# A seven-product block scheme for the gate and up products of an encoder's feed-forward layers

## The chip, the cores and the metric

The kernel runs on one core of a Trainium2 chip. The metric is the device time of one execution in microseconds (us). The engines work side by side, each through its own queue in order: TensorE (PE in the profile, its weight loads PEld), VectorE (DVE), ScalarE (ACT), GpSimd (POOL), and SyncE (SP), which here only issues transfers.

## The reference

Two macaron layers over 512 tokens of 1024 features. Each layer is a feed-forward block (FFN), a mixer of pooling, Fourier and attention heads, and a second FFN; a last norm follows. What the change touches is the FFN:

```python
D_MODEL, SEQ, DEPTH, D_FF = 1024, 512, 2, 2816

def rmsnorm(x, g):
    xf = x.astype(jnp.float32)
    y = xf * lax.rsqrt(jnp.mean(xf * xf, axis=-1, keepdims=True) + NORM_EPS)
    return (y * g.astype(jnp.float32)).astype(x.dtype)

def swiglu(x, w_gate, w_up, w_down):
    return (jax.nn.silu(x @ w_gate) * (x @ w_up)) @ w_down

for l in range(DEPTH):
    x = x + 0.5 * swiglu(rmsnorm(x, ffn1_norm[l]), ffn1_w_gate[l], ffn1_w_up[l], ffn1_w_down[l])
    x = x + mixers(rmsnorm(x, mix_norm[l])) @ w_out[l]
    x = x + 0.5 * swiglu(rmsnorm(x, ffn2_norm[l]), ffn2_w_gate[l], ffn2_w_up[l], ffn2_w_down[l])
```

## The kernel before, in words

Activations lie transposed: X[k] (k = 0 to 7) holds 128 features on the partitions and all 512 tokens along the free axis. Weights are the stationary operand of every projection. A float32 product is carried by three passes of float32r: each operand is split into a part hi and a rest lo, and hi x hi, hi x lo and lo x hi are added up in PSUM (mm3, L87). split() (L83) makes hi by a copy on ScalarE (L84) and lo by a subtraction on VectorE, in some places of the mixers on GpSimd (L85). The norm's gain is multiplied into x ahead of the product (Norm.scaled, L225); the factor per token, nm.r, is applied where sums leave PSUM. It comes from squares on ScalarE (L236), their sum on GpSimd (L240), two products with a matrix of ones and a chain of small VectorE steps (rsqrt, L183 to L209).

An FFN (ffn, L301) runs over two halves of the 2816 hidden features, 11 columns of 128 each. Per column a weight tile of 1 MB, gate and up side by side, is loaded and split, and pair() (L291) makes 2 x 8 x 3 matmuls of 128x128 by 128x512 into two PSUM banks. Then VectorE multiplies both banks by nm.r (L317, L319), ScalarE takes Silu (L318), VectorE multiplies gate by up (L320), and the result is split into ah and al. After 11 columns come eight down products (dn, L325 to L334) of 11 x 3 matmuls each, which are added to X[m]; in the second half each new X[m] is fed to the next norm at once.

The weights form one stream: weights() (L131) issues loads two items ahead and splits one item ahead. Staging has two buffers of 1 MB, hi and lo four of 0.5 MB each, work tiles 64 of 0.25 MB. [...] The mixers follow a list of steps written by hand (ORDER). [...]

Of the kernel before, what the change touches and what calls it, by code (L numbers as in the profile page):

```python
# [16 lines left out]
F32 = mybir.dt.float32  # L17
# [10 lines left out]
L = 2  # L28
DFF = 2816
NF = DFF // P  # L30
HALF = NF // 2
KT = D // P
NH = 4
# [4 lines left out]
NG = 64  # L38
# [9 lines left out]
# What runs on VectorE (or, for the row scale of the scores, ScalarE) rather than on GpSimd.  # L48
# [4 lines left out]
def build(tc, xt, gu, dn, qk, wv, wfa, wo, pw, fw, small, lamv, alibi, dft_c, dft_s, out):  # L53
# [3 lines left out]
    with (  # L57
        tc.tile_pool(name="const", bufs=1) as cp,
        tc.tile_pool(name="stage", bufs=2) as stp,
        tc.tile_pool(name="whi", bufs=4) as whp,  # L60
        tc.tile_pool(name="wlo", bufs=4) as wlp,
# [31 lines left out]
        items = []  # L93
        for l in range(L):
            for n in range(2):
                i = 2 * l + n
                if n:
                    src = {f"P{h}": qk[l, h] for h in range(NH)}
                    src |= {"V0": wv[l, 0], "V1": wv[l, 1], "A": wfa[l, 1], "F": wfa[l, 0]}
                    src |= {"W0a": wo[l, 0], "W1a": wo[l, 1], "W2": wo[l, 2], "W3": wo[l, 3]}  # L100
                    items += [(src[x], 2048, V if x in ON_VECTOR else G) for x in ORDER if x in src]
                for hf in range(2):
                    items += [(gu[i, hf * HALF + c], 2048, V) for c in range(HALF)]
                    items += [(dn[i, hf, m], HALF * P, V) for m in range(KT)]
        staged, ready = {}, {}
        pos = [0, 0, 0]

        def w_load(i, parts=1):
            src, w, _ = items[i]
            st = stp.tile([P, 2048], F32, tag="st", name=f"st{i}")  # L110
            q = w // parts
            for j in range(parts):
                nc.sync.dma_start(st[:, j * q : (j + 1) * q], src[:, j * q : (j + 1) * q])
            staged[i] = st

        def w_split(i, parts=1):
            _, w, eng = items[i]
            st = staged.pop(i)
            h = 1024 if w == 2048 else 6 * P
            res = []  # L120
            for n, (a, b) in enumerate(((0, h), (h, w))):
                hi = whp.tile([P, 1024], F32R, tag="hi", name=f"hi{i}_{n}")
                lo = wlp.tile([P, 1024], F32R, tag="lo", name=f"lo{i}_{n}")
                q = (b - a) // parts
                for j in range(parts):
                    s = slice(j * q, (j + 1) * q)
                    split(st[:, a + j * q : a + (j + 1) * q], hi[:, s], lo[:, s], eng)
                res += [hi, lo]
            ready[i] = res

        def weights():  # L131
            i = pos[0]
            pos[0] += 1
            while pos[1] < min(len(items), i + 3):
                w_load(pos[1])
                pos[1] += 1
            while pos[2] < min(len(items), i + 2):
                w_split(pos[2])
                pos[2] += 1
            return ready.pop(i)  # L140

# [4 lines left out]
        st0 = stp.tile([P, 2048], F32, tag="st", name="st0")  # L146
        for k in range(KT):
            nc.sync.dma_start(X[k], xt[k])
            if k % 2 == 0:
                s = slice(k * 256, (k + 2) * 256)  # L150
                nc.sync.dma_start(st0[:, s], items[0][0][:, s])
        staged[0] = st0
        pos[1] = 1
        w_load(1)
        pos[1] = 2
# [9 lines left out]
        # TensorE's clock rises while it works: products of zeros until the first weights are there.  # L165
# [11 lines left out]
        # 1/sqrt(-2 v): an exponent guess, a Newton step and a step of third order, scaled so that  # L177
        # each step ends in one (t + c) * y.
# [38 lines left out]
        class Norm:  # L217
# [7 lines left out]
            def scaled(self, k, act=False):  # L225
                gain = sm[:, self.c + k : self.c + k + 1]
                self.h[k], self.l[k] = g(F32R, name="xh"), g(F32R, name="xl")
                if act:
                    A.activation(self.h[k], X[k], AF.Copy, scale=gain)
                else:  # L230
                    V.tensor_scalar(self.h[k], X[k], gain, None, MUL)
# [15 lines left out]

        class Final:
            """The last RMSNorm: the sums over features as columns, tokens on partitions."""
# [41 lines left out]
        def pair(b, w, rh, rl, ks=range(KT), steps=((0, 4), (4, 7), (7, 8))):  # L291
            """Two tiles of outputs; k in the order of arrival, the last one at the end."""
# [8 lines left out]
        def ffn(nm, nxt, first=False):  # L301
            for hf in range(2):
                ah, alo = [], []
                for c in range(HALF):
                    w = weights()
                    b = [bank("gate"), bank("up")]
                    if first and hf == 0 and c == 0:
                        pair(b, w, nm.h, nm.l, steps=[(k, k + 1) for k in range(KT)])
                        for k in range(KT):
                            nm.squared(k)  # L310
                        held = b
                        continue
                    pair(b, w, nm.h, nm.l)
                    nm.end()
                    for b in [held, b] if first and hf == 0 and c == 1 else [b]:
                        t1, t2 = g(name="t1"), g(name="t2")
                        V.tensor_tensor(t1, b[0], nm.r, MUL)  # L317
                        A.activation(t1, t1, AF.Silu)  # L318
                        V.tensor_tensor(t2, b[1], nm.r, MUL)  # L319
                        V.tensor_tensor(t1, t1, t2, MUL)  # L320
                        h, lo = g(F32R, name="ah"), g(F32R, name="al")
                        split(t1, h, lo)
                        ah.append(h)
                        alo.append(lo)
                for m in range(KT):  # L325
                    w = weights()
                    b = bank("dn")
                    for j in range(HALF):
                        wh, wl = (w[0], w[1]) if j < 6 else (w[2], w[3])
                        s = slice((j % 6) * P, (j % 6 + 1) * P)  # L330
                        mm3(b, wh[:, s], wl[:, s], ah[j], alo[j], j == 0, j == HALF - 1)
                    V.scalar_tensor_tensor(X[m], b, 0.5, X[m], MUL, ADD)
                    if hf:
                        nxt.feed(m)  # L334

# [1 line left out]
        def mixer(l, nm, nxt):  # L337
# [131 lines left out]
            # pooling: window sums by doubling  # L469
# [45 lines left out]
            # Fourier: fold positions s and 512 - s, apply channels, then positions  # L515
# [117 lines left out]
        nm = Norm(C_FFN1)  # L633
        for k in range(KT):
            if k % 4 == 0:
# [109 lines left out]
```

## Time and profile before

| | |
|---|---|
| three runs | 1897.64, 1899.21, 1900.34 us; median 1899.21 us |
| span of the profiled execution | 1896.2 us; its time is not given apart from its span |
| TensorE busy | 1850.6 us (98%), 8057 matmuls |
| VectorE busy | 1034.7 us (55%) |
| ScalarE busy | 657.2 us (35%) |
| GpSimd busy | 162.9 us (9%) |
| HBM read | 168.82 MB, 90 GB/s over the span |

All durations come from one profiled execution, and sums are made against its span. In a row of groups stand the line, the engine, the operation, output and inputs by the program's names, the shape and the count, then total busy time in us and the mean of one in ns, then the idle time in front of them and what ended it. A row of the timeline starts with start and duration in us; several instructions merged into one row carry their count. In a row of stretches each engine's busy time stands with its number of instructions, and PEclk is the granted clock of TensorE as a share of full speed. An instruction that is held up while it runs shows a longer duration. A matmul's duration is its whole passage, and consecutive ones overlap.

### The profile page before, as it was taken

The numbers are of one execution on the slowest core, as the hardware profiler recorded it, in microseconds if no ns is written. First come the engines' busy times: TensorE is split into PE (matmuls) and PEld (weight loads), VectorE is DVE, ScalarE is ACT, GpSimd is POOL, SyncE is SP. The second block draws the span as 40 slices with busy tenths as digits, with TensorE's granted clock in tenths as the row PEclk, the third lists the DMA queues.
The fourth block names the chain that finished last, engine by engine and source line by source line (L and its number), as shares of the span: only waits on it lengthen the run. The fifth ranks groups of instructions, "written<-read, shape, count | busy, mean of one in ns | idle before, by whom it ended". The sixth has DMA issues, their size and how long they took to land.

```text
span 1896.2 us, 19973 instructions
## 1 busy us (share of the span) xinstructions
PE 1850.6 (98%) x8057; PEld 1496.7 (79%) x8057; DVE 1034.7 (55%) x1535; ACT 657.2 (35%) x960; POOL 162.9 (9%) x106
## 2 busy tenths in 40 slices
PE   9999999999799999999999999999998999999997
PEld 7888888877688888888888888888776888888886
DVE  6543444588788443444654334445988864334433
ACT  5322222367443222232322222322764432223232
POOL 2000000213211000000100000002232200000001
PEclk9999999999899999999999999999999999999998
DMA  5223222322103213222322232223221132232221
GB/s 193 107 72 113 93 97 74 114 86 92 45 23 114 109 61 108 109 89 77 112 101 93 76 120 89 84 90 111 86 70 45 67 111 82 77 120 89 87 87 60
DMA packets 31053, 172.21 MB, mean 91 GB/s; under 512 B 3568, under 2 KB 5616, under 8 KB 16752
## 3 DMA queue, kind: packets, MB, share of 16 engines
q1 hardware_dynamic: 27792, 167.25, 24.8%
q10 hardware_dynamic: 3168, 3.68, 0.6%
q8 instruction: 63, 1.03, 0.2%
q14 instruction: 30, 0.25, 0.0%
HBM read 168.82 MB, written 2.10 MB: 90 GB/s over the span
## 4 chain that ended last, share of the span: by engine, by line
PE 87%; DVE 8%; ACT 3%; issue 1%; DMA 0%; SPq 0%; DVEq 0%; ACTq 0%
PE gate L88 9%; PE up L88 9%; PE dn L90 9%; PE up L90 9%; PE dn L89 9%; PE gate L90 9%; PE up L89 9%; PE dn L88 9%; PE gate L89 9%; DVE sc L394 1%; PE wo L89 1%; PE wo L88 1%; PE wo L90 1%; PE pp L89 1%; PE pp L88 1%; PE pp L90 1%
## 5 line engine op out<-in xcount | busy, mean ns | idle before, releaser
L84 ACT ACTIVATE hi<-st 128x1024 fp32r<-128x1024 f32 (+2 forms) x358 | 339.4, 950 | 951.4 <-PE up L89 549.7
L85 DVE TENSOR_TENSOR lo<-st,hi 128x1024 fp32r<-128x1024 f32 (+2 forms) x326 | 356.7, 1096 | 366.5 <-ACT hi L84 366.5
L88 PE MATMUL gate<-xh,hi 128*128 128x512 f32 x704 | 277.6, 394 | 1.6 <-ACT hi L84 1.6
L88 PE MATMUL up<-xh,hi 128*128 128x512 f32 x704 | 277.4, 394 | 0.0
L90 PE MATMUL up<-xh,lo 128*128 128x512 f32 x704 | 277.3, 394 | 0.0
L90 PE MATMUL dn<-ah,lo 128*128 128x512 f32 x704 | 277.1, 394 | 0.0
L89 PE MATMUL dn<-al,hi 128*128 128x512 f32 x704 | 277.1, 394 | 0.0
L90 PE MATMUL gate<-xh,lo 128*128 128x512 f32 x704 | 276.9, 393 | 0.0
L89 PE MATMUL up<-xl,hi 128*128 128x512 f32 x704 | 276.7, 393 | 0.0
L88 PE MATMUL dn<-ah,hi 128*128 128x512 f32 x704 | 276.7, 393 | 0.0
L89 PE MATMUL gate<-xl,hi 128*128 128x512 f32 x704 | 276.7, 393 | 0.0
L317 DVE TENSOR_TENSOR t<-gate,y 128x512 f32<-128x512 f32 x88 | 60.8, 691 | 219.5 <-PE gate L90 219.4
L88 PEld LDWEIGHTS gate<-xh,hi 128*128 128x128 f32 x704 | 132.4, 188 | 32.9 <-ACT hi L84 2.3
L90 PEld LDWEIGHTS up<-xh,lo 128*128 128x128 f32 x704 | 132.2, 188 | 31.1
L90 PEld LDWEIGHTS gate<-xh,lo 128*128 128x128 f32 x704 | 132.3, 188 | 31.0
L89 PEld LDWEIGHTS up<-xl,hi 128*128 128x128 f32 x704 | 132.3, 188 | 30.8
L89 PEld LDWEIGHTS dn<-al,hi 128*128 128x128 f32 x704 | 132.2, 188 | 30.9
L89 PEld LDWEIGHTS gate<-xl,hi 128*128 128x128 f32 x704 | 132.3, 188 | 30.8
L88 PEld LDWEIGHTS dn<-ah,hi 128*128 128x128 f32 x704 | 132.2, 188 | 30.8
L90 PEld LDWEIGHTS dn<-ah,lo 128*128 128x128 f32 x704 | 132.3, 188 | 30.3
L88 PEld LDWEIGHTS up<-xh,hi 128*128 128x128 f32 x704 | 132.4, 188 | 30.0
L240 POOL TENSOR_TENSOR sq<-sq,sq 128x512 f32<-128x512 f32 x36 | 56.1, 1557 | 1109.8 <-ACT sq L236 1096.9
(212 smaller groups left out, 2078.1 us busy)
## 6 DMA issues: line engine op xcount, KB each, us to landing
st<-in_gu SPq DMA_DIRECT2D x87, 1024.0 KB, 4.8
st<-in_dn SPq DMA_DIRECT2D x64, 704.0 KB, 4.0
st<-in_qk SPq DMA_DIRECT2D x8, 1024.0 KB, 4.8
st<-in_wo SPq DMA_DIRECT2D x8, 1024.0 KB, 4.9
st<-in_wv SPq DMA_DIRECT2D x4, 1024.0 KB, 4.9
st<-in_wfa SPq DMA_DIRECT2D x4, 1024.0 KB, 4.9
x<-in_xt SPq DMA_DIRECT2D x8, 256.0 KB, 5.4
tab<-in_dft_s ACTq DMA_DIRECT2D x10, 129.0 KB, 3.0
```

Of the source, the lines that this page charges most:

```text
L84: A.activation(hi, src, AF.Copy)
L85: (lo_eng or V).tensor_tensor(lo, src, f(hi), SUB)
L88: T.matmul(o, lh, rh, start=start, stop=False)
L89: T.matmul(o, lh, rl, start=False, stop=False)
L90: T.matmul(o, ll, rh, start=False, stop=stop)
L240: (V if k == KT - 1 else G).tensor_tensor(self.acc, self.acc, sq, ADD)
L317: V.tensor_tensor(t1, b[0], nm.r, MUL)
L394: V.scalar_tensor_tensor(sc[0], sc[1], rc[:, 2:3], sc[0], MUL, ADD)
```

## The change

**The block scheme.** Two columns of gate and up are now one unit. For a unit the product of a 2x2 block matrix of weights (rows: the two columns of 128 outputs; block columns: even and odd feature blocks) and a 2x2 block matrix of activations (even and odd feature blocks by first and second 256 tokens) is formed by seven block products in place of eight. Each product takes one weight operand of 128 x 1024, and sums the four pairs of feature blocks for gate and up (z) side by side in one bank: 4 x 2 x 3 matmuls of 128x128 by 128x256. Four of the seven weight operands are sums of blocks; produce() makes them on GpSimd (L160 of the changed kernel) from the loaded tiles, or from an earlier sum, and all seven are split as before. On the side of the activations PairNorm.scaled makes, for each pair of feature blocks, two scaled copies on ScalarE, the differences ta and tb in four VectorE instructions of 256 tokens, and splits one of 256 and three of 512 columns.

**Putting the results together.** VectorE forms y, v, w22, w12 and w21 from the banks qa, qe, qb, qg and earlier parts. The factor r is applied by two instructions on VectorE and two on GpSimd (L405, L406), which write the halves of t[0] and t[1]; then Silu, product and split for each of the two columns.

**The rest.** An FFN has three chunks of 4, 4 and 3 units, each followed by eight down products over 8, 8 or 6 columns; PSUM results are added to X after every chunk. Weights are loaded in tiles of 0.5 MB into six buffers, sums have two, hi and lo three each, work tiles 56 in place of 64. Operands are split two ahead. The mixers' code is as before.

```diff
+CHUNKS = ((0, 4), (4, 8), (8, 11))
+TH = S // 2
+AHEAD = 2
+RAWS = 4
-        tc.tile_pool(name="stage", bufs=2) as stp,
-        tc.tile_pool(name="whi", bufs=4) as whp,
-        tc.tile_pool(name="wlo", bufs=4) as wlp,
+        tc.tile_pool(name="stage", bufs=6) as stp,
+        tc.tile_pool(name="sums", bufs=2) as smp,
+        tc.tile_pool(name="whi", bufs=3) as whp,
+        tc.tile_pool(name="wlo", bufs=3) as wlp,
+        tc.tile_pool(name="act", bufs=2) as atp,
...
+                for c0, c1 in CHUNKS:
+                    for u in range(c0, c1):
+                        a11, a21, a22, a12 = [raw(gu[i, u][:, q * 1024 : (q + 1) * 1024]) for q in range(4)]
+                        operand_of(a11)
+                        l5 = operand_of(a21, plus=a22)
+                        l6 = operand_of(l5, plus=a11)
+                        operand_of(a11, plus=a21)
+                        operand_of(a12)
+                        operand_of(l6, plus=a12)
+                        operand_of(a22)
+                    for m in range(KT):
+                        w = 2 * (c1 - c0) * P
+                        operand_of(raw(dn[i, m][:, 2 * c0 * P : 2 * c1 * P], w), w)
...
+        def produce(i, parts=1):
+            src, plus, w, eng = recipes[i]
+            load(max([x[1] for x in (src, plus) if x and x[0] == "r"] + [-1]) + RAWS)
+            t = tiles[src]
+            if plus:
+                t = smp.tile([P, 1024], F32, tag="sum", name=f"sum{i}")
+                G.tensor_tensor(t, tiles[src], tiles[plus], ADD)
+                tiles["s", i] = t
...
+            def scaled(self, k):
+                gain = sm[:, self.c + k : self.c + k + 1]
+                self.b[k] = g(name="xg")
+                A.activation(self.b[k], X[k], AF.Copy, scale=gain)
+                if k % 2 == 0:
+                    return
+                b1, b2 = self.b.pop(k - 1), self.b.pop(k)
+                c0, c1 = slice(0, TH), slice(TH, S)
+                ta, tb = g(name="ta"), g(name="tb")
+                V.tensor_tensor(ta[:, c0], b1[:, c0], b1[:, c1], SUB)
+                V.tensor_tensor(ta[:, c1], b1[:, c1], b2[:, c1], SUB)
+                V.tensor_tensor(tb[:, c0], ta[:, c1], b1[:, c0], SUB)
+                V.tensor_tensor(tb[:, c1], b2[:, c0], tb[:, c0], ADD)
+                one = g(F32R, name="xo")
+                split(b1[:, c0], one[:, c0], one[:, c1])
+                res = {1: (one[:, c0], one[:, c1])}
+                for src, js in ((ta, (5, 7)), (tb, (6, 4)), (b2, (2, 3))):
+                    hi, lo = g(F32R, name="xh"), g(F32R, name="xl")
+                    split(src, hi, lo)
...
+                    def product(q, j, start, stop):
+                        wh, wl = operand()
+                        for p in range(NK):
+                            xh, xl = nm.x[p][j]
+                            for z in range(2):
+                                s = slice((2 * p + z) * P, (2 * p + z + 1) * P)
+                                o = q[:, z * TH : (z + 1) * TH]
+                                k = {"skip_group_check": True}
+                                T.matmul(o, wh[:, s], xh, start=start and p == 0 and z == 0, stop=False, **k)
+                                T.matmul(o, wl[:, s], xh, start=False, stop=False, **k)
+                                T.matmul(o, wh[:, s], xl, start=False, stop=stop and p == NK - 1 and z == 1, **k)
+                    product(qa, 1, True, True)
...
+                    q1 = g(name="q1")
+                    A.activation(q1, qa, AF.Copy)
+                    product(qe, 5, True, True)
+                    product(qb, 6, True, True)
+                    product(qg, 7, True, True)
+                    nm.end()
...
+                    V.tensor_tensor(y, qb, q1, ADD)
+                    V.tensor_tensor(v, qe, y, ADD)
+                    V.tensor_tensor(w22, qg, v, SUB)
+                    product(qa, 2, False, True)
+                    product(qe, 3, False, True)
+                    product(qg, 4, False, True)
...
+                    V.tensor_tensor(t[0][:, :, 0:TH], halves(qa), r[0], MUL)
+                    V.tensor_tensor(w12, qe, y, ADD)
+                    G.tensor_tensor(t[0][:, :, TH:S], halves(w12), r[1], MUL)
+                    G.tensor_tensor(t[1][:, :, TH:S], halves(w22), r[1], MUL)
+                    V.tensor_tensor(w21, qg, y, SUB)
+                    V.tensor_tensor(t[1][:, :, 0:TH], halves(w21), r[0], MUL)
+                    for x in t:
+                        A.activation(x[:, 0], x[:, 0], AF.Silu)
+                        V.tensor_tensor(x[:, 0], x[:, 0], x[:, 1], MUL)
+                        h, lo = g(F32R, name="ah"), g(F32R, name="al")
+                        split(x[:, 0], h, lo)
```

**The order on VectorE.** Before, two columns in the middle of a half of the first FFN: lo is half a weight tile, t with gate and up are the two products with nm.r, t with t is gate by up, al the rest of the result.

```order
L85 TENSOR_TENSOR lo_0_574<-st_501,hi_0_573 128x1024
L317 TENSOR_TENSOR t_61_561<-gate_511,y_331 128x512
L319 TENSOR_TENSOR t_62_562<-up_512,y_331 128x512
L85 TENSOR_TENSOR lo_1_578<-st_501,hi_1_577 128x1024
L320 TENSOR_TENSOR t_61_561<-t_61_561,t_62_562 128x512
L85 TENSOR_TENSOR al_568<-t_61_561,ah_567 128x512
L85 TENSOR_TENSOR lo_0_644<-st_571,hi_0_643 128x1024
L317 TENSOR_TENSOR t_67_631<-gate_581,y_331 128x512
L319 TENSOR_TENSOR t_68_632<-up_582,y_331 128x512
L85 TENSOR_TENSOR lo_1_648<-st_571,hi_1_647 128x1024
L320 TENSOR_TENSOR t_67_631<-t_67_631,t_68_632 128x512
L85 TENSOR_TENSOR al_638<-t_67_631,ah_637 128x512
```

Now, in the first chunk of the first FFN, from w12 of one unit (w_99; w_100 is w21, t_0 and t_1 are t[0] and t[1], y_412 is nm.r) to the next unit's fifth lo and its y. lo from sum tiles are the splits of sums:

```order
L404 TENSOR_TENSOR w_99_1014<-qe_789,y_914 128x512
L101 TENSOR_TENSOR lo_985<-sum_982,hi_984 128x1024
L411 TENSOR_TENSOR t_0_1012<-t_0_1012 128x512
L407 TENSOR_TENSOR w_100_1015<-qg_791,y_914 128x512
L408 TENSOR_TENSOR t_1_1013<-w_100_1015,y_412 128x2x256
L101 TENSOR_TENSOR lo_1041<-sum_1038,hi_1040 128x1024
L101 TENSOR_TENSOR al_1025<-t_0_1012,ah_1024 128x512
L411 TENSOR_TENSOR t_1_1013<-t_1_1013 128x512
L101 TENSOR_TENSOR lo_1073<-sum_1070,hi_1072 128x1024
L101 TENSOR_TENSOR al_1031<-t_1_1013,ah_1030 128x512
L101 TENSOR_TENSOR lo_1103<-st_948,hi_1102 128x1024
L391 TENSOR_TENSOR y_1160<-qb_1036,q_109_1068 128x512
```

The tail of a unit now stands between the second and the fifth lo of the next one; behind these rows v, the sixth lo, w22, the seventh lo, t_0 and the next unit's first lo follow.

**The order on GpSimd.** Before, the only instructions in the FFNs are the sums of squares of the norms; those of the norm ahead of the first FFN (sq_239) and of the next norm (sq_2170) follow each other directly:

```order
L240 TENSOR_TENSOR sq_239<-sq_239,sq_250 128x512
L240 TENSOR_TENSOR sq_239<-sq_239,sq_253 128x512
L240 TENSOR_TENSOR sq_239<-sq_239,sq_256 128x512
L240 TENSOR_TENSOR sq_2170<-sq_2170,sq_2221 128x512
L240 TENSOR_TENSOR sq_2170<-sq_2170,sq_2273 128x512
```

Now, for the same units as above: two sums of the next unit, two products with r of this one, the other two sums of the next unit, and the products of that one.

```order
L160 TENSOR_TENSOR sum_982<-st_734,st_854 128x1024
L160 TENSOR_TENSOR sum_1038<-sum_982,st_732 128x1024
L406 TENSOR_TENSOR t_1_1013<-w_98_916,y_412 128x2x256
L405 TENSOR_TENSOR t_0_1012<-w_99_1014,y_412 128x2x256
L160 TENSOR_TENSOR sum_1070<-st_732,st_734 128x1024
L160 TENSOR_TENSOR sum_1130<-sum_1038,st_948 128x1024
L406 TENSOR_TENSOR t_1_1255<-w_112_1162,y_412 128x2x256
L405 TENSOR_TENSOR t_0_1254<-w_113_1256,y_412 128x2x256
```

Six instructions per unit, all of which read two SBUF tiles, now run on GpSimd where none did.

More of the change, by code (lines that the diff above doesn't have):

```diff
@@ L37 @@
 NT = S // 2 + 2
-NG = 64
+NG = 56
 NWARM = 5
@@ L100, in build @@
                     src |= {"W0a": wo[l, 0], "W1a": wo[l, 1], "W2": wo[l, 2], "W3": wo[l, 3]}
[L101 to L105, printed above, removed]
[L106 to L110 removed]
+                    for x in ORDER:
+                        if x in src:
+                            for z in range(2):
+                                operand_of(raw(src[x][:, z * 1024 : (z + 1) * 1024]), eng=V if x in ON_VECTOR else G)
@@ new lines, in build, with load @@
+        tiles, ready = {}, {}
+        pos = [0, 0, 0]
+        def load(upto):
+            while pos[1] < min(len(raws), upto):
+                src, w = raws[pos[1]]
+                st = stp.tile([P, 1024], F32, tag="st", name=f"st{pos[1]}")
+                nc.sync.dma_start(st[:, 0:w], src)
+                tiles["r", pos[1]] = st
+                pos[1] += 1
+        def produce(i, parts=1):
[6 more added lines that the diff above has]
+                tiles["s", i] = t
+            hi = whp.tile([P, 1024], F32R, tag="hi", name=f"hi{i}")
+            lo = wlp.tile([P, 1024], F32R, tag="lo", name=f"lo{i}")
@@ L131, in weights, with operand @@
-        def weights():
+                s = slice(j * q, (j + 1) * q)
+                split(t[:, s], hi[:, s], lo[:, s], eng)
+            ready[i] = hi, lo
+        def operand():
             i = pos[0]
             pos[0] += 1
[L134 to L138, printed above, removed]
+            while pos[2] < min(len(recipes), i + AHEAD + 1):
+                produce(pos[2])
@@ L139, in weights @@
                 pos[2] += 1
             return ready.pop(i)
+        def weights():
+            return (*operand(), *operand())
         sm = cp.tile([P, NSMALL], F32, name="sm")
@@ L301, in ffn @@
         def ffn(nm, nxt, first=False):
-            for hf in range(2):
+            for c0, c1 in CHUNKS:
                 ah, alo = [], []
[L304 to L308, printed above, removed]
+                for u in range(c0, c1):
+                    qa, qe, qb, qg = bank("qa"), bank("qe"), bank("qb"), bank("qg")
+                    def product(q, j, start, stop):
+                        wh, wl = operand()
+                        for p in range(NK):
+                            xh, xl = nm.x[p][j]
+                            for z in range(2):
+                                s = slice((2 * p + z) * P, (2 * p + z + 1) * P)
[5 more added lines that the diff above has]
+                    product(qa, 1, True, True)
+                    if first and u == 0:
@@ new lines, in ffn, with halves @@
+                    V.tensor_tensor(w22, qg, v, SUB)
+                    product(qa, 2, False, True)
+                    product(qe, 3, False, True)
+                    product(qg, 4, False, True)
+                    t = [atp.tile([P, 2, S], F32, tag="t", name=f"t{cnt[0]}_{i}") for i in range(2)]
+                    w12, w21 = g(name="w12"), g(name="w21")
+                    def halves(x):
+                        return x.rearrange("p (z n) -> p z n", z=2)
+                    V.tensor_tensor(t[0][:, :, 0:TH], halves(qa), r[0], MUL)
@@ L321, in ffn @@
                         h, lo = g(F32R, name="ah"), g(F32R, name="al")
-                        split(t1, h, lo)
+                        split(x[:, 0], h, lo)
                         ah.append(h)
                         alo.append(lo)
+                n = 2 * (c1 - c0)
                 for m in range(KT):
-                    w = weights()
+                    wh, wl = operand()
                     b = bank("dn")
[L328 to L331, printed above, removed]
+                    for j in range(n):
+                        s = slice(j * P, (j + 1) * P)
+                        mm3(b, wh[:, s], wl[:, s], ah[j], alo[j], j == 0, j == n - 1)
```

98 lines of the change are left out of this document (38 added, 60 removed).

## Prediction

> **What bounds the kernel now.** I read the totals first, then stretches, then single instructions.
>
> ```profile
> PE 1850.6 (98%) x8057; PEld 1496.7 (79%) x8057; DVE 1034.7 (55%) x1535; ACT 657.2 (35%) x960; POOL 162.9 (9%) x106
> ```
>
> TensorE (PE) is busy for 98% of the span, and GpSimd (POOL) for 9%. By stretch:
>
> ```profile
> core 0: us, PE busy (x) PEld busy (x) DVE busy (x) ACT busy (x) POOL busy (x), PEclk, DMA share, GB/s
> 140.00:300.00 160.00, 160.00 (x695) 130.09 (x694) 65.30 (x76) 42.49 (x51) 0.00 (x0) 1.00 0.28 100
> 505.10:509.40 4.30, 0.40 (x2) 0.00 (x0) 4.17 (x10) 0.00 (x0) 1.13 (x1) 0.81 0.47 154
> 509.50:514.20 4.70, 4.70 (x11) 3.71 (x12) 1.46 (x3) 0.63 (x1) 0.00 (x0) 0.50 0.17 70
> ```
>
> The first row lies inside a feed-forward block (FFN): TensorE never waits there, VectorE (DVE) works 41% of it, GpSimd not at all. The other two lie in a mixer and return below. So in the FFNs the time is the number of matmuls times their spacing. Starts of matmuls stand in the timeline; first and last of 49 in a row, 512 wide, exactly one pair() of gate and up products apart:
>
> ```profile
> 99.77 0.39 PE L88 MATMUL up<-xh,hi 128*128 128x512 f32 x1
> ...
> 110.85 0.39 PE L88 MATMUL up<-xh,hi 128*128 128x512 f32 x1
> ```
>
> 11.08 us for 48 makes 0.231 us each (the 0.39 is one matmul's whole passage; they overlap). Two weight columns of 128, which the new kernel makes in one unit, take 22.2 us.
>
> **The change part by part.** *Matmuls.* A unit has 7 products x 4 blocks x 2 x 3 passes = 168 matmuls 256 wide, where 96 were 512 wide. The Fourier step has that shape, each with its own weight load; first and last of 12 in a row:
>
> ```profile
> 532.96 0.28 PE L88 MATMUL FG<-g,eh 128*128 128x256 f32 x1
> ...
> 534.26 0.28 PE L90 MATMUL FG<-g,zl 128*128 128x256 f32 x1
> ```
>
> 1.30 us for 11 steps is 0.118 us, so the weight load stays hidden and a unit costs TensorE 19.8 us: 2.4 us less, 104 us over 44 units (4 FFNs x 11), if the others keep up. A product is 2.8 us. The down products are 528 x 0.231 us per FFN as before: no change.
>
> *The other engines.* The rows that price them:
>
> ```profile
> L85 DVE TENSOR_TENSOR lo<-st,hi 128x1024 fp32r<-128x1024 f32 x190 | 240.1, 1264 | 206.7 <-ACT hi L84 206.7
> L85 DVE TENSOR_TENSOR al<-t,ah 128x512 fp32r<-128x512 f32 x88 | 60.9, 692 | 60.4 <-ACT ah L84 60.4
> L84 ACT ACTIVATE hi<-st 128x1024 fp32r<-128x1024 f32 x222 | 235.0, 1060 | 583.5 <-PE up L89 437.3 <-PE dn L89 67.7 <-PE pp L89 41.7
> L318 ACT ACTIVATE t<-t 128x512 f32<-128x512 f32 x88 | 54.2, 616 | 12.6 <-DVE t L317 12.6
> L85 POOL TENSOR_TENSOR lo<-st,hi 128x1024 fp32r<-128x1024 f32 x32 | 79.8, 2493 | 163.0 <-ACT hi L84 141.9 <-DVE t L207 20.6 <-POOL yl L85 0.5
> L265 POOL TENSOR_TENSOR sq<-sq,sq 128x512 f32<-128x512 f32 x6 | 7.7, 1292 | 350.6 <-ACT sq L258 350.6
> ```
>
> ScalarE has per unit 7 copies hi of 1.06, q1, two Silu and two ah of about 0.62: 10.5 us of 19.8, no bound. VectorE has 18 instructions: 7 of 1024 and 11 of 512. Back to back they start closer than they last:
>
> ```profile
> 25.30 2.35 DVE L85 TENSOR_TENSOR lo<-st,hi 128x1024 fp32r<-128x1024 f32 x2
> ...
> 28.17 1.22 DVE L85 TENSOR_TENSOR lo<-st,hi 128x1024 fp32r<-128x1024 f32 x1
> ```
>
> 2.35 - 1.22 = 1.13 us each. And four of 512 that read PSUM, beside a GpSimd subtraction:
>
> ```profile
> 465.29 2.40 POOL L85 TENSOR_TENSOR lo<-st,hi 128x1024 fp32r<-128x1024 f32 x1 [2.73 <-ACT hi L84]
> ...
> 466.54 2.48 DVE L85 TENSOR_TENSOR tl<-T,th 128x512 fp32r<-128x512 f32 x4 [1.19 <-ACT th L84]
> ```
>
> (2.48 - 0.69) / 3 = 0.60 us, unhindered. VectorE's own work is 7 x 1.13 + 11 x 0.60 = 14.5 us. GpSimd has four sums of 1024 (2.40) and two products of 512 (1.29): 12.2 us. Each fits into 19.8; together they don't, for this reason:
>
> ```profile
> 419.86 0.75 DVE L394 SCALAR_TENSOR_TENSOR sc<-sc,rc,sc 128x512 f32<-128x512 f32 x1
> 420.20 2.67 POOL L85 TENSOR_TENSOR lo<-st,hi 128x1024 fp32r<-128x1024 f32 x1 [0.91 <-ACT hi L84]
> 420.53 2.89 DVE L363 TENSOR_TENSOR kl<-tk,kh 64x512 fp32r<-64x512 f32 x1
> ```
> ```profile
> 568.33 1.21 DVE L85 TENSOR_TENSOR lo<-st,hi 128x1024 fp32r<-128x1024 f32 x1
> 568.94 1.75 POOL L240 TENSOR_TENSOR sq<-sq,sq 128x512 f32<-128x512 f32 x1 [2.67 <-ACT sq L236]
> 569.47 1.78 DVE L232 SCALAR_TENSOR_TENSOR xl<-x,sm,xh 128x512 fp32r<-128x512 f32 x1
> ```
>
> A VectorE instruction with both inputs in SBUF and a GpSimd instruction exclude each other: sc ends at 420.61 and GpSimd 2.26 us later, then kl 0.55 us after GpSimd. In the second set lo ends at 569.54, GpSimd 1.15 us later, xl 0.56 after that. So, handed over at once, the place between them is held 2.26 or 1.16 us by GpSimd, 0.55 by a 512 and about 1.09 by a 1024 of VectorE.
>
> [...]
>
> Per unit 7 lo and 5 of the 512 (t1, two gate-by-up products, two al) read SBUF twice: 10.4 us; GpSimd 4 x 2.26 + 2 x 1.16 = 11.4 us. The sum, 21.8 us, is the floor of a steady unit. Its ceiling, nothing beside GpSimd, is 14.5 + 12.2 = 26.7 us. Between them the queues decide. I walked a unit through both printed orders (own time; waits in brackets): w12 0.60, lo 1.13, [3.42: t_0 on GpSimd, then the third sum, 1.16 + 2.26], gate-by-up 0.55, w21 0.60, t_1 0.60, lo 1.13, al 0.60, [2.26: fourth sum], gate-by-up 0.55, lo 1.13, al 0.60, [2.26: next unit's first sum], lo 1.09, y 0.60, v 0.60, lo 1.13, w22 0.60, [1.66: next unit's second sum, begun beside w22], lo 1.09, t_0 0.60, [0.55: rest of t_1 on GpSimd], lo 1.09. Own 14.3, waits 10.1: 24.4 us, VectorE never waiting for TensorE. Behind each blocked instruction stand the next lo, for which TensorE's next product waits, and the reads of PSUM, for which GpSimd's next t waits. I take 24.4: it follows the rows and the printed order, while floor and ceiling each need the order to be something else.
>
> A chunk's units differ. The first finds two operands split and two or three sums made under the down products: TensorE sets 19.8. In the second VectorE's lag builds up: 22.9. In the last no sums are made ahead (2.26 + 1.66 less): 20.5. Chunks of four take 19.8 + 22.9 + 24.4 + 20.5 = 87.6 us, of three 63.2; an FFN 2 x 87.6 + 63.2 = 238.4 against 11 x 22.2 = 243.8, so 5.4 less, 21 us for four. At 21.8 a unit it would be about 78 us less, at 26.7 about 50 more.
>
> *Ends of chunks* (12, where 8 were): the last al comes some 5.7 us after the last product, after two Silu and two splits in turn; the matmuls put in front cover 5.5. I take 0.4 each: 5 us, 0 to 20.
>
> *Starts of FFNs.* Every pair of feature blocks now takes five VectorE instructions of 256 and three of 512, and the chain of the row norm follows, both in the queue ahead of the first units' lo:
>
> ```profile
> L85 DVE TENSOR_TENSOR lo<-st,hi 128x256 fp32r<-128x256 f32 x8 | 3.0, 420 | 0.9 <-ACT hi L84 0.9
> L203 DVE TENSOR_TENSOR t<-t,v 128x512 f32<-128x512 f32 x14 | 9.7, 690 | 3.2 <-ACT t L197 2.9
> ```
>
> Last pair 5 x 0.34 + 3 x 0.60 = 3.5, norm eight instructions of 0.69 with two around it, 6.7: 10 us, until now covered by dense matmuls with VectorE idle. First units have little room for it: 9 us at three starts (0 to 15), 27 us. At the kernel's start all four pairs, 14 us, and 2 MB of weights instead of 1 MB stand before the second product can end: 15 us (5 to 25).
>
> *No cost:* loads are the same bytes in halves, six buffers deep; in the mixers three split buffers where four were, covered by a projection's 48 x 0.231 = 11 us. If those covers fail, some us in each mixer. With TensorE's stops (below) I allow 8 us.
>
> Sum: 1896.2 - 21 + 5 + 27 + 15 + 8 = 1930 us of span. The median of the runs, 1899.2, is 3 above the profiled span: **1933 us**.
>
> **The rivals.** *A, TensorE keeps the pace:* the collisions fall into waits, a unit costs 19.8; -104 with half of the start terms, +20: 1815 us. For it speaks that each engine alone has room; against it the floor of 21.8. 0.13. *B, as forecast, but the hand-overs fall better:* a unit near 22.3, -65 instead of -21, with starts half as dear (21): 1868 us. 0.22. *C, TensorE's clock falls too:* in the walk it waits up to 3.6 us between a unit's second and third product. In the mixer, behind 4.3 us of near idleness, 11 matmuls of 512 took 4.70 us, 0.427 each, at a granted clock of 0.50. A product at half clock costs 2.8 us more; in each of some 20 steady units that is +56: 1985 us. 0.18; it decides once such waits are regular.
>
> [...]
>
> *D, narrow matmuls aren't half:* above 22.2 / 168 = 0.132 us nothing is gained at all; at 0.140 a unit is 23.5, 1.3 x 44 = 57 us dearer, with the starts some 1975 us. The 12 in a row speak against it. 0.05.
>
> **How the numbers follow.** The forecast has 0.42, and 1893 to 1965 as its own range. About 0.2% (4 us) is what measuring this kernel can tell. Faster: A, most of B (0.20) and 0.01 of the forecast, 0.34; same: the upper end of B and the lower end of the forecast, 0.05; slower: the rest, C and D, 0.61. The range leaves out A and the far ends of C and D: 1845 to 1995. It also takes in the bounds of the steady unit with the other terms as summed (1933 - 57 to 1933 + 71) but for 9 us at the top.
>
> **What would show it.** Right: GpSimd busy near 12 us of each unit, lo on VectorE often 2 to 3.4 us instead of 1.22, TensorE waiting for lo inside units, steady units of 24 us, first ones of 20. Wrong: TensorE dense in the chunks (A), steady units under 22.5 us (B), a granted clock of 0.5 in chunks (C), matmuls over 0.13 us apart (D).

## The result and the profile after

| | before | after |
|---|---|---|
| median of four runs | 1898.43 us (1897.20 to 1900.34) | 2020.14 us (2018.94 to 2021.49) |
| span of the profiled execution | 1896.2 us | 2017.4 us |

The ratio is 1.0641, with a 95% interval of 1.0625 to 1.0656: slower by 122 us. The forecast was 1933 us, in a range that ended at 1995.

The totals of the changed kernel, on the page of its profile:

```profile
PE 1824.6 (90%) x11225; PEld 1616.0 (80%) x11225; DVE 1569.1 (78%) x1868; ACT 851.5 (42%) x1189; POOL 823.6 (41%) x370
```

TensorE's busy time fell by only 26 us and its share from 98% to 90%; VectorE's rose by 534 us and GpSimd's by 661. The groups that grew, with total and mean:

```profile
L101 DVE TENSOR_TENSOR lo<-st,hi 128x1024 fp32r<-128x1024 f32 x211 | 426.5, 2021 | 33.0 <-ACT hi L100 33.0
L101 DVE TENSOR_TENSOR lo<-sum,hi 128x1024 fp32r<-128x1024 f32 x176 | 241.7, 1373 | 26.4 <-ACT hi L100 26.4
L160 POOL TENSOR_TENSOR sum<-st,st 128x1024 f32<-128x1024 f32 x88 | 242.9, 2760 | 393.7 <-DVE lo L101 208.8 <-DMA st<-in_gu 163.5 <-ACT hi L100 18.8
L406 POOL TENSOR_TENSOR t<-w,y 128x512 f32<-128x512 f32 x44 | 97.4, 2214 | 53.3 <-DVE w L393 53.3
```

A subtraction lo of a loaded tile lasts 2.02 us on average where it lasted 1.26 (one of a sum 1.37), a product with r on GpSimd 2.21 where 1.29 was the price of its size. The four units of a middle chunk of the first FFN (the second of three), cut at the first matmul of each, then the first chunk, a middle chunk and eight down products of the second FFN, in the view of stretches:

```profile
178.02:197.89 19.87, 19.87 (x170) 19.87 (x168) 16.03 (x13) 7.91 (x8) 10.91 (x5) 1.00 0.33 107
197.89:221.02 23.13, 20.98 (x170) 20.16 (x169) 20.81 (x19) 9.99 (x12) 14.67 (x6) 1.00 0.31 90
221.02:244.76 23.74, 21.94 (x170) 21.53 (x169) 21.43 (x19) 10.10 (x12) 15.27 (x6) 0.93 0.29 90
244.76:267.21 22.45, 20.40 (x171) 20.00 (x169) 19.81 (x19) 9.99 (x12) 10.92 (x5) 1.00 0.35 105
...
621.90:731.72 109.82, 91.53 (x676) 87.58 (x674) 102.78 (x95) 46.39 (x60) 59.47 (x26) 0.92 0.26 79
...
777.92:867.14 89.22, 82.00 (x673) 79.96 (x672) 78.09 (x67) 37.89 (x44) 51.78 (x21) 1.00 0.31 97
...
731.72:777.92 46.20, 44.90 (x194) 35.80 (x193) 20.44 (x21) 10.79 (x12) 8.91 (x4) 1.00 0.28 87
```

The number behind each stretch is its length; PE, PEld, DVE, ACT and POOL follow, then the granted clock. A middle chunk takes 89.2 us for four units, 22.3 each: the 22.2 that two columns took before. A first chunk takes 20.6 us more, with TensorE at a clock of 0.92. Cut in the same way from first matmul to first matmul, the whole span gives this sum:

| term | forecast | measured |
|---|---|---|
| units of all chunks, first chunks counted like middle ones | -21 | +1 |
| ends of chunks (down products) | +5 | +19 |
| three starts of FFNs (20.6, 18.0, 21.6; before 0.8, 0.5, 1.0) | +27 | +58 |
| the kernel's start (34.4 and 1.8 until the first matmul; before 1.9) | +15 | +34 |
| both mixers (207.9 and 206.2; before 204.0 and 201.0) | +8 | +9 |
| sum | +34 | +121 |

### The profile page after: what moved, and what is told of

Same layout as the page of the kernel before. It is cut to its first block, busy times and chain, and to the rows that moved or that the text cites. A ratio compares the mean times of both kernels' runs of the same rounds, so it can differ in the third digit from the quotient of the medians.

```text
span 2017.4 us, 27780 instructions
## 1 busy us (share of the span) xinstructions
PE 1824.6 (90%) x11225; PEld 1616.0 (80%) x11225; DVE 1569.1 (78%) x1868; ACT 851.5 (42%) x1189; POOL 823.6 (41%) x370
## 5 line engine op out<-in xcount | busy, mean ns | idle before, releaser
L160 POOL TENSOR_TENSOR sum<-st,st 128x1024 f32<-128x1024 f32 x88 | 242.9, 2760 | 393.7 <-DVE lo L101 208.8
L160 POOL TENSOR_TENSOR sum<-sum,st 128x1024 f32<-128x1024 f32 x88 | 233.5, 2653 | 289.0 <-DVE lo L101 232.0
L100 ACT ACTIVATE hi<-sum 128x1024 fp32r<-128x1024 f32 x176 | 185.5, 1054 | 260.3 <-PE qe L377 91.6
L101 DVE TENSOR_TENSOR lo<-sum,hi 128x1024 fp32r<-128x1024 f32 x176 | 241.7, 1373 | 26.4 <-ACT hi L100 26.4
L375 PE MATMUL qe<-xh,hi 128*128 128x256 f32 x704 | 205.1, 291 | 10.8 <-ACT hi L100 5.5
L376 PE MATMUL qe<-xh,lo 128*128 128x256 f32 x704 | 205.9, 292 | 8.8 <-DVE lo L101 8.8
L376 PE MATMUL qg<-xh,lo 128*128 128x256 f32 x704 | 200.8, 285 | 12.7 <-DVE lo L101 12.6
L377 PE MATMUL qe<-xl,hi 128*128 128x256 f32 x704 | 204.4, 290 | 0.0
L375 PE MATMUL qg<-xh,hi 128*128 128x256 f32 x704 | 198.6, 282 | 0.0
L377 PE MATMUL qg<-xl,hi 128*128 128x256 f32 x704 | 198.2, 282 | 0.0
```

What stands on the lines that cost most here:

```text
L100: A.activation(hi, src, AF.Copy)
L101: (lo_eng or V).tensor_tensor(lo, src, f(hi), SUB)
L160: G.tensor_tensor(t, tiles[src], tiles[plus], ADD)
L375: T.matmul(o, wh[:, s], xh, start=start and p == 0 and z == 0, stop=False, **k)
L376: T.matmul(o, wl[:, s], xh, start=False, stop=False, **k)
L377: T.matmul(o, wh[:, s], xl, start=False, stop=stop and p == NK - 1 and z == 1, **k)
```

## The experiments

The theory behind the forecast was that GpSimd and VectorE instructions with two SBUF inputs shut each other out (below: the lock). Its rivals: VectorE's own load is the bound and GpSimd a real help; or the chain from a sum over hi and lo to the product is too long.

**The sums left out.** In produce() the second tile takes the sum's place:

```diff
-                t = smp.tile([P, 1024], F32, tag="sum", name=f"sum{i}")
-                G.tensor_tensor(t, tiles[src], tiles[plus], ADD)
-                tiles["s", i] = t
+                t = tiles["s", i] = tiles[plus]
```

> The changed kernel with the weight sums left out: where a sum was made on GpSimd, the second loaded tile is split in its place, so the gate and up products are of other weights; everything else stays, the two products with r on GpSimd too. Exclusion theory (GpSimd and two-SBUF-input work of VectorE shut each other out): per unit only 2 x 1.16 us of GpSimd are left beside 10.4 us of VectorE, so TensorE sets the pace: steady units 19.9 to 20.5 us in place of 23.7, a middle chunk of four about 80 us in place of 89.2, an FFN's two later chunks and its first 25 us less together, four FFNs 100 us, the starts some 10 us besides: 1910 us (1890 to 1935). Rival (VectorE's own work and the chain from w12 over Silu to al are the bound, GpSimd only looks busy): VectorE's instructions are all still there, so units stay above 22 us and the time is 1975 us or more.

Measured: 1857.58 us, ratio to the kernel before 0.9785 (0.9769 to 0.9802). A middle chunk:

```profile
715.38:794.82 79.44, 79.44 (x674) 79.43 (x673) 65.34 (x67) 38.80 (x45) 10.36 (x8) 1.00 0.37 113
```

TensorE is dense, 19.86 us per unit, with all of VectorE's own instructions in place: its own load isn't the bound of a unit, and a narrow matmul does cost half a wide one (TensorE's 168 at 0.118 us, the wide ones before at 0.231). The time fell 163 us, beyond the expected range: 104 in the units, and besides the excess of the first chunks halved (90.1, 82.2, 90.0 and 102.2 us against 79.4), and the ends of chunks lost 8. Here the lock and the wait for the sums are gone together; the next run parts them.

**The same sums, but nobody waits for them.** The sums are made as in the changed kernel, and the split still takes the second tile:

```diff
                 tiles["s", i] = t
+                t = tiles[plus]
```

> As the run without sums (1858 us: the second loaded tile is split in the place of each sum), but GpSimd still makes the four sums per unit, into tiles that nobody reads but the next sum: no engine waits for their values. It tells the shutting out of VectorE from the length of the chain sum, hi, lo, product. Exclusion: VectorE still loses 2.26 us to each sum, 10.4 + 2 x 1.16 + 4 x 2.26 = 21.8 us per unit: a middle chunk of four 85 to 90 us, 1960 to 2020 us. Chain: units stay at 19.85, a middle chunk at 79.4, 1858 to 1880 us.

Measured: 2030.28 us, ratio 1.0696 (1.0677 to 1.0716): slower even than the changed kernel and above the expected range. A middle chunk takes 90.9 us, and its timeline shows the lock by itself:

```profile
841.54 3.07 POOL L160 TENSOR_TENSOR sum<-st,st 128x1024 f32<-128x1024 f32 x1 [7.60 <-DMA st<-in_gu]
844.68 3.27 POOL L160 TENSOR_TENSOR sum<-sum,st 128x1024 f32<-128x1024 f32 x1
846.32 2.72 DVE L101 TENSOR_TENSOR lo<-st,hi 128x1024 fp32r<-128x1024 f32 x1
848.03 3.25 POOL L160 TENSOR_TENSOR sum<-st,st 128x1024 f32<-128x1024 f32 x1
849.56 2.81 DVE L101 TENSOR_TENSOR lo<-st,hi 128x1024 fp32r<-128x1024 f32 x1
851.37 3.27 POOL L160 TENSOR_TENSOR sum<-sum,st 128x1024 f32<-128x1024 f32 x1
852.90 2.82 DVE L101 TENSOR_TENSOR lo<-st,hi 128x1024 fp32r<-128x1024 f32 x1
...
854.60 2.26 POOL L407 TENSOR_TENSOR t<-w,y 128x512 f32<-128x512 f32 x1
856.82 1.28 POOL L406 TENSOR_TENSOR t<-w,y 128x512 f32<-128x512 f32 x1
...
858.80 0.69 DVE L412 TENSOR_TENSOR t<-t 128x512 f32<-128x512 f32 x1 [3.08 <-ACT t L411]
```

Sum and lo alternate, one pair each 3.34 us: the 2.26 and 1.09 that the forecast took from single hand-overs. No product needs these sums, so the length of a chain through them can't be what costs. They still hold the loaded tiles that they read; so do the sums on VectorE in the run after this one, where TensorE keeps its pace. The unit's 22.7 us are not the lock alone (21.8), though: the train starts late, when a tile is loaded (first row), the products with r stand behind all four sums in GpSimd's queue, and VectorE waits 3.1 us for the Silu behind them (last row).

**All on VectorE.** Both products with r and the sums:

```diff
-                G.tensor_tensor(t, tiles[src], tiles[plus], ADD)
+                V.tensor_tensor(t, tiles[src], tiles[plus], ADD)
...
-                    G.tensor_tensor(t[0][:, :, TH:S], halves(w12), r[1], MUL)
-                    G.tensor_tensor(t[1][:, :, TH:S], halves(w22), r[1], MUL)
+                    V.tensor_tensor(t[0][:, :, TH:S], halves(w12), r[1], MUL)
+                    V.tensor_tensor(t[1][:, :, TH:S], halves(w22), r[1], MUL)
```

> The four sums and both products with r of a unit moved from GpSimd to VectorE, nothing left out. Exclusion theory: a sum costs 1.13 us on VectorE and shuts VectorE out for 2.26 on GpSimd, so although VectorE gets 14.5 + 4 x 1.13 + 2 x 0.60 = 20.2 us of own work, a steady unit falls from 23.7 to 20.2 to 21.0 us; a chunk of four about 83 us in place of 89.2, four FFNs some 70 us less, and the starts and the kernel's start a little cheaper: 1940 us (1915 to 1960). Rival (VectorE's own load is the bound, and GpSimd's help is real): 5.7 us more per unit, steady units of 27 us or more, 44 units: slower than the changed kernel, 2150 us.

Measured: 1898.98 us, ratio 1.0003 (0.9994 to 1.0013). So 121 us come back by taking the help away, more than the expected range allowed. The second FFN's first and middle chunk:

```profile
591.71:691.26 99.55, 87.97 (x675) 84.84 (x674) 94.23 (x117) 47.20 (x60) 7.19 (x4) 0.95 0.29 89
735.69:814.78 79.09, 79.09 (x673) 79.09 (x672) 75.76 (x89) 39.12 (x45) 0.00 (x0) 1.00 0.35 111
```

VectorE does six more instructions per unit, and in a middle chunk is busy 75.8 us where it was 78.1 with help: the work is cheaper than the waiting. TensorE is dense in middle chunks, and the ends of chunks cost nothing more (44.4 to 44.8 us). But the first chunks still exceed the middle ones by some 20, 17, 20 and 33 us. These starts are a cause of their own.

**Only the products with r on VectorE.** Of the diff above, the last four lines.

> Only the two products with r moved from GpSimd to VectorE; the four sums stay on GpSimd. Exclusion theory: a product holds 0.55 us on VectorE and 1.16 on GpSimd, so the sum of what excludes falls from 21.8 to 10.4 + 2 x 0.55 + 4 x 2.26 = 20.5 us, and Silu of the first column no longer waits for GpSimd's turn (VectorE waited 1.85 us for it in each steady unit): units of 21.5 to 22.5 us in place of 23.7, 44 units some 50 us less: 1970 us (1945 to 1990). Rival (VectorE's own load): 1.2 us more per unit, 2060 us. Third possibility, that the sums alone set the turn: within 10 us of 2020.

Measured: 1968.02 us, ratio 1.0368 (1.0352 to 1.0383), a middle chunk 85.68 us, 21.4 per unit, just under the 21.5 to 22.5 that the lock gave. Moving two of GpSimd's six instructions is worth 52 us.

**Two down products interleaved at a chunk's start.**

```diff
+                    todo = [(q, j) for js in (range(n - 2), (n - 2,), (n - 1,)) for q in (0, 1) for j in js]
+                    for q, j in todo if m == 1 else [(m, j) for j in range(n)]:
```

> The changed kernel with the first two down products of each chunk interleaved: all columns but the last two for both, then these for both, so that 11 us of matmuls (8 in a chunk of three) instead of 5.5 stand between a chunk's last gate and up product and the first use of the last column's result. If the 1.85 us by which eight down products exceed their matmuls (46.2 against 192 x 0.231 = 44.35) are the wait for the last al, they go: 12 x 1.85 = 22 us less, 1998 us (1994 to 2004). If the excess has another cause, or the wait moves to the next operand of the stream: within 6 us of 2020.

Measured: 1999.88 us, ratio 1.0537 (1.0521 to 1.0553). In the changed kernel TensorE stood twice in the first down products of a chunk (44.90 us busy of 46.20 in the last of the stretches above; these rows are from the second chunk of the first FFN):

```profile
272.55 0.50 PE L105 MATMUL dn<-al,hi 128*128 128x512 f32 x1 [0.78 <-DVE al L101]
272.88 0.40 PE L106 MATMUL dn<-ah,lo 128*128 128x512 f32 x1
273.81 0.73 PE L104 MATMUL dn<-ah,hi 128*128 128x512 f32 x2 [0.53 <-ACT ah L100]
```

With two products interleaved the same stretch is dense:

```profile
729.11:773.45 44.34, 44.34 (x195) 36.03 (x194) 18.69 (x21) 10.68 (x12) 8.04 (x4) 1.00 0.29 92
```

20 us for twelve ends: the wait for the last column's result, as expected.

**What makes the starts dear.** First the norm left out, then the differences. The norm:

```diff
+            def squared(self, k):
+                pass
+
+            def end(self):
+                if self.r is None:
+                    self.r = g(name="r1")
+                    V.memset(self.r, 1.0)
```

> The changed kernel with the norm ahead of each FFN left out except for its gain: no squares, no sums of them, no products with ones, no rsqrt chain; r is a tile of ones. (The norms of the mixers stay.) It splits the excess of the first chunks over the middle ones (34.4, 20.6, 18.0 and 21.6 us; 94.6 in all). If the norm's chain in VectorE's queue is half of it, as the prediction had it (6.7 us of some 10), and TensorE's wait for the squares besides: about 10 us less per start, 1980 us (1965 to 1995). If the norm hides beside products 2 to 4 of the first unit and the pairs' differences or the first operands make the excess: within 10 us of 2020.

Measured: 1962.33 us, ratio 1.0332 (1.0317 to 1.0347), just below the expected range. The first chunk of the second FFN:

```profile
610.20:704.55 94.35, 84.33 (x674) 81.73 (x672) 87.34 (x85) 43.79 (x54) 51.22 (x21) 0.98 0.30 92
```

It is 15.5 us shorter than with the norm (109.82), the others 14.9, 16.6 and, at the kernel's start, 11.7: 59 us in all.

The differences:

```diff
-                ta, tb = g(name="ta"), g(name="tb")
-                V.tensor_tensor(ta[:, c0], b1[:, c0], b1[:, c1], SUB)
-                V.tensor_tensor(ta[:, c1], b1[:, c1], b2[:, c1], SUB)
-                V.tensor_tensor(tb[:, c0], ta[:, c1], b1[:, c0], SUB)
-                V.tensor_tensor(tb[:, c1], b2[:, c0], tb[:, c0], ADD)
+                ta, tb = b1, b2
```

> The changed kernel with the four VectorE instructions per pair that form ta and tb left out; the scaled blocks themselves are split in their place, so the seven products are of other operands. At the start at 620 us the last two pairs' eight instructions lasted 2.63, 1.50, 0.89, 0.41, and 4 x 0.41. If they stand on the path: 4 to 6 us less per start, about 2000 us (1990 to 2008). If the queue behind them (splits, norm, lo) sets the end anyway: within 8 us of 2020.

Measured: 1999.75 us, ratio 1.0537 (1.0521 to 1.0553); the first chunks are 4.5, 4.7, 5.4 and 3.6 us shorter, as expected. So of the 20.6 us of the second FFN's start the norm is some 15 and the differences some 5, each taken out by itself. At the kernel's start, with its 34.4, they are 12 and 4, and the rest was not taken apart.

**The first unit made the old way.** On top of the version with all on VectorE: the first unit of each FFN uses four plain weight operands and 96 wide matmuls, scaled() only splits, and the differences come in a method of their own behind these matmuls.

```diff
+                        if u == 0:
+                            for q in (0, 3, 1, 2):
+                                operand_of(raw(gu[i, u][:, q * 1024 : (q + 1) * 1024]))
+                            continue
...
+            def pairs(self, k):
...
+                            order = [(k, z) for q in ((0, 2), (2, 4), (4, 6), (6, 7), (7, 8)) for z in range(2) for k in range(*q)]
...
+                        for k in range(1, KT, 2):
+                            nm.pairs(k)
```

> All sums and products with r on VectorE, and the first unit of each FFN made the old way: 96 matmuls of 512, four weight operands without sums, and the pairs' differences only made while these matmuls run. Nothing is left out. A first unit then costs 22.2 us of TensorE in place of 19.9, and needs of the norm's input only the plain splits. If the excess of the first chunks (33.1, 20.3, 17.0 and 20.5 us with everything on VectorE) is work that has to come before the first product can end, it falls to about 8 us each and 15 at the kernel's start: 1899 - 50 = 1850 us (1830 to 1870). Rival: the work is only moved, VectorE's queue in the first chunk is as long as before, and the chunk ends when it is done: 1885 us or more.

Measured: 1877.45 us, ratio 0.9892 (0.9876 to 0.9909): between the two. The first chunks fell to 94.1, 96.1 and 94.0 us, and 107.0 at the kernel's start: the first unit was dense at the second FFN, and TensorE's waits came in the second unit, behind the pairs. Of the excess over the matmuls some 12 to 14 us of 17 to 20 were left: most of the work had only been moved.

**Two units.** The same with two old units per FFN, the pairs' differences spread over them; at the kernel's start the norm's end moves behind both rows of the first unit (not in these lines).

```diff
-                        if u == 0:
+                        if u < OLD:
...
+                            if u == 1 and row == 0:
+                                nm.pairs(5)
+                                nm.pairs(7)
```

> As the version with the first unit of each FFN made the old way (1877 us), but with two such units, the pairs' differences spread over both, and at the kernel's start the norm's end behind both rows of the first unit. Nothing is left out. An old unit costs TensorE 2.35 us more. With one, the first chunks still exceeded their matmuls (79.3 + 2.35) by 12.4, 14.4, 12.3 us and 25 at the kernel's start. If that is still VectorE's queue of the first 50 us (pairs, norm, operands with sums), another 22 us of wide matmuls with little VectorE work take up most of it: the excess falls to 4 each and 14 at the start, less 35 and plus 9.4 for the old units: 1850 us (1840 to 1865). Rival, the rest is fixed (the norm's chain and TensorE's lower clock behind it): 1877 + 9 = 1886 us.

Measured: 1843.60 us, ratio 0.9715 (0.9702 to 0.9728). The kernel's first chunk and the second FFN's:

```profile
8.58:110.21 101.63, 93.10 (x530) 81.48 (x531) 80.20 (x113) 49.46 (x70) 8.22 (x6) 0.95 0.37 127
579.77:664.47 84.70, 84.70 (x532) 76.19 (x531) 75.76 (x106) 41.50 (x53) 1.30 (x1) 1.00 0.30 94
```

At the second FFN TensorE is dense from the first matmul at a clock of 1.00, and 84.7 is 79.3 + 2 x 2.35 within 0.7. This version beats the kernel before by 2.85%. The kernel's start still takes 17 us more than another start.

**The norm's end later at the kernel's start.**

```diff
-                            if row == 0:
+                            if row == int(first):
                                 nm.end()
```

> As the version with the first unit old (1877 us), but in the first FFN the norm's end stands behind both rows of the first unit. There TensorE stood still for 10.8 us in front of the product with ones, between the first and the second row. If that wait is for the squares alone, the second row's 48 matmuls (11.1 us) fill it: 8 to 11 us less, 1868 us. Rival, the second row waits for its own operands, which are queued behind the squares and the pairs on ScalarE and VectorE: within 3 us of 1877.

Measured: 1881.95 us, ratio 0.9914 (0.9901 to 0.9928), 4.5 us slower than with the end in front. The first chunk, which alone is made in another order, took 108.9 us where it took 107.0; the rest of the difference lies in stages that both make alike and shows nothing of the edit. Neither theory holds. The wait was filled, the second row ran through. Then:

```profile
36.45 0.40 PE L250 MATMUL ss<-g,ones 128*128 128x512 f32 x1
...
44.14 0.38 PE L412 MATMUL qe<-xh,hi 128*128 128x256 f32 x1 [3.55 <-ACT xh L100]
...
46.01 0.58 PE L412 MATMUL qb<-xh,hi 128*128 128x256 f32 x1 [1.38 <-ACT xh L100]
```

The pairs stand behind the norm's end in the program; put later, it made them late, and the second unit waited for their splits. That is half of the account. This chunk with the end late, and below it with the end in front:

```profile
9.34:118.26 108.92, 96.52 (x602) 87.85 (x603) 92.89 (x125) 52.98 (x74) 9.96 (x6) 0.91 0.33 116
8.36:115.36 107.00, 89.56 (x603) 80.60 (x603) 92.86 (x124) 52.45 (x73) 9.78 (x6) 0.95 0.35 121
```

TensorE waited 12.4 us in place of 17.4, but its matmuls took 7.0 us longer, at a mean clock of 0.91 in place of 0.95: the wait was shortened by 5 us, and the clock took back more.

## Why the prediction was wrong

The direction and the mechanism were right, the size was a quarter to a third of what came: +34 forecast, +121 measured. By the steps:

*The lock.* Right. The unit in the third place shows the stops of the walk, in the timeline of VectorE and GpSimd:

```profile
221.05 2.21 POOL L405 TENSOR_TENSOR t<-w,y 128x512 f32<-128x512 f32 x1 [1.76 <-DVE w L404]
223.22 2.41 POOL L160 TENSOR_TENSOR sum<-st,st 128x1024 f32<-128x1024 f32 x1
223.96 2.21 DVE L411 TENSOR_TENSOR t<-t 128x512 f32<-128x512 f32 x1 [1.86 <-ACT t L410]
...
231.96 2.93 DVE L101 TENSOR_TENSOR lo<-st,hi 128x1024 fp32r<-128x1024 f32 x1 [0.39 <-ACT hi L100]
...
236.14 2.11 DVE L101 TENSOR_TENSOR lo<-sum,hi 128x1024 fp32r<-128x1024 f32 x1
...
238.78 3.10 DVE L101 TENSOR_TENSOR lo<-st,hi 128x1024 fp32r<-128x1024 f32 x1
...
242.40 1.73 DVE L101 TENSOR_TENSOR lo<-st,hi 128x1024 fp32r<-128x1024 f32 x1
```

Behind w12 the walk had a stop of 3.42 us; here VectorE idles 1.86 and the gate-by-up product lasts 1.53 longer than its 0.68, 3.39 together. The other stops differ in place (1.7, 0.9, 1.9 and 0.5 us on the four lo, beyond their own 1.22), and the unit took 23.7 us where 24.4 was said. First, second, third: 19.9, 23.1, 23.7 against 19.8, 22.9, 24.4. The alternation in the run with idle sums, one pair in 3.34 us, agrees: with nothing shut out it was expected to keep the 19.85 us per unit of the run without sums; it took 22.7.

*The last unit of a chunk* was set at 20.5 and took 22.5. No sums are made ahead in it, but the stop behind w12 carried over from the unit before, and TensorE still waited 1.7 us in one piece in its third product. With 0.2 us more in second units and 0.7 less in third ones this turned -21 into nothing.

*Ends of chunks*, 0.4 us each: 1.85. The last al ended 7.4 us after the last product's last matmul (267.1 to 274.5 in the first FFN), not 5.7: Silu of the first column waited for a product with r on GpSimd:

```profile
268.07 0.63 ACT L410 ACTIVATE t<-t 128x512 f32<-128x512 f32 x1 [2.44 <-POOL t L405]
```

And the cover was less than 5.5: of the first down product's 24 matmuls 21 stand in front of the first use of the last column, 21 x 0.231 = 4.9 us. With these products on VectorE eight down products take 44.9 to 45.3 us, and with the sums there too 44.4 to 44.8, where 46.2 stood.

*The starts* are the step that failed most: "Last pair ... 3.5, norm ... 6.7: 10 us ... 9 us at three starts (0 to 15)", and 15 (5 to 25) at the kernel's start. Measured: 19 on average and 34, outside both bounds. The mis-sized term is the norm: priced at 6.7, it was worth some 15 when it was left out. The pairs were too low as well: their differences alone, of all pairs, were some 5 where 3.5 stood for the whole last pair. The norm was priced by its own instructions, but in VectorE's one queue it shares the turn with the first units' lo, and both wait for GpSimd:

```profile
638.15 3.44 DVE L101 TENSOR_TENSOR lo<-st,hi 128x1024 fp32r<-128x1024 f32 x1
641.51 2.82 DVE L270 TENSOR_TENSOR sq<-sq,sq 128x512 f32<-128x512 f32 x1
...
646.00 3.40 DVE L101 TENSOR_TENSOR lo<-st,hi 128x1024 fp32r<-128x1024 f32 x1
```

The row of the last sum of squares in the kernel before, and TensorE's two longest waits in this chunk now:

```profile
L240 DVE TENSOR_TENSOR sq<-sq,sq 128x512 f32<-128x512 f32 x6 | 4.1, 687 | 3.9 <-POOL sq L240 3.9
...
627.90 0.39 PE L377 MATMUL qa<-xo,hi 128*128 128x256 f32 x1 [3.62 <-DVE xo L101]
645.05 0.79 PE L246 MATMUL ss<-g,ones 128*128 128x512 f32 x1 [3.02 <-ACT g L100]
```

The last sum of squares took 2.82 in place of 0.69, TensorE stood 3.02 us for it (and 3.62 before that for the split of a pair), and its clock fell: in the stretch around the sum,

```profile
640.50:660.35 19.85, 13.75 (x77) 12.75 (x76) 18.59 (x20) 4.75 (x5) 5.99 (x4) 0.74 0.17 54
```

0.74 was granted on average. For the same matmuls TensorE was busy 91.5 us in the first chunk and 82.0 in a middle one (82.0 at a clock of 0.92 would be 89): of the 20.6 us about half are matmuls that take longer, the rest is more waiting. The first half was nowhere in the sum. Rival C had this loss, but put it into steady units, where the clock stayed at 0.93 to 1.00; the waits there are 1.7 us, not 3.6. GpSimd's turns are not needed for this loss: with sums and products on VectorE the first chunks exceed the middle ones by as much (20, 17 and 20 us). What both have is VectorE's full queue: busy 102.8 of 109.8 us in the one case and 94.2 of 99.6 in the other. With two old units in front it was 75.8 of 84.7, and TensorE was dense. How much would go if the clock alone stayed up was not tried, nor deeper buffers for hi and lo.

*The rivals.* A needed GpSimd's sums away: without them TensorE did keep the pace, and starts, ends of chunks and mixers then left 1858, not 1815. B fell: steady units took 23.7 us, and the starts were twice as dear as forecast, not half. D fell too, with 0.118 us between narrow matmuls in the dense stretches. (C's price of 56 us on top of the forecast makes 1989, not 1985.)

*The range.* Its top was made of the units' bounds, with the starts as summed. All five terms of the sum erred to the same side. The likeliest reason, argued and not tested by itself, is that all hung on one thing, a full queue on VectorE, and were added as if each had a cover of its own.

## What to carry to other kernels

Before work is given to GpSimd to relieve VectorE, look at where both read: here a GpSimd sum of two SBUF tiles kept a VectorE instruction with two SBUF inputs out for 2.26 of its 2.40 us, twice the 1.13 us, from its start to the next, that VectorE needed for the same sum, so the help cost more than the work. When an engine's queue is nearly full (here VectorE's, busy 102.8 of 109.8 us in a first chunk), price what is put in front of a stage by the whole stretch until the queue has caught up, not by the instructions added, and with the clock that TensorE was granted there (here 0.92, and 1.00 in a middle chunk). A scheme that saves matmuls but needs more preparation can gain in the steady part and lose at the starts: here, with all sums on VectorE, a middle chunk took 79.1 us, where four times the 22.2 of before are 88.8, and the first chunks 17 to 33 us more than a middle one. The first two units in the old form took most of that loss away (1843.6 us against 1897.5 for the kernel before).

## What the runs showed of the hardware

GpSimd's and VectorE's instructions did not share the lock by chance or by shares: over a train of sums and subtractions they took strict turns, one pair in 3.34 us (the run with idle sums, 844.68 to 851.37). GpSimd held it 2.26 us for 128x1024 (kernel before, 420.61 to 422.87). Undisturbed, a sum of that size lasted 2.40 us on GpSimd (changed kernel, at 214.64) and 1.22 on VectorE (all on VectorE, at 609.72), 1.97 to 1.

TensorE's granted clock was 0.74 on average over a stretch of 20 us in which it was busy for 13.75 and waited 3.0 us at the most in one piece. Cut finer, it was 0.50 in some parts and 1.00 in others:

```profile
642.90:649.70 6.80, 4.65 (x20) 4.46 (x21) 6.80 (x5) 1.58 (x2) 3.59 (x2) 0.50 0.19 67
653.10:656.50 3.40, 3.40 (x16) 3.40 (x17) 3.40 (x5) 0.00 (x0) 0.00 (x0) 0.50 0.00 0
656.60:660.30 3.70, 3.70 (x33) 3.70 (x33) 2.59 (x4) 1.06 (x1) 0.02 (x1) 1.00 0.02 4
```

A much shorter wait than rival C's 3.6 us can come ahead of such a fall, or not. Of two units in a row with nearly the same longest wait, in the middle chunk shown above, the first had a mean clock of 0.93 and the second one of 1.00:

```profile
228.69 0.38 PE L376 MATMUL qb<-xh,lo 128*128 128x256 f32 x1 [1.72 <-DVE lo L101]
...
252.44 0.39 PE L376 MATMUL qb<-xh,lo 128*128 128x256 f32 x1 [1.73 <-DVE lo L101]
```
